# Seven products instead of eight in six of sixteen blocks of an MLP's second product

## The chip, the cores and the metric

The kernel runs on one NeuronCore of a Trainium2 chip. The metric is device time in microseconds for one execution. The core has a matrix engine (PE, TensorE), which reads its stationary and moving operands from on-chip SBUF and writes sums to one of eight PSUM banks of 128 x 512 float32 values; a vector engine (DVE, VectorE), a scalar engine (ACT, ScalarE) and a general one (POOL, GpSimd); and queues that move data from the chip's main memory (issued by SP here). Every engine takes its own instructions in order, and they wait for each other by semaphores.

## The reference

The program is a decoder of two layers on 256 tokens of width 1024. Each layer has attention (of two different kinds, which the change doesn't touch) and an MLP with a squared ReLU:

```
def rms_norm(x, g):
    y = x * rsqrt(mean(x * x, axis=-1) + 1e-5)
    return y * g

def sqrelu_mlp(x, w1, w2):
    h = relu(x @ w1)
    return (h * h) @ w2

h = h + attention(rms_norm(h, g0))
h = h + sqrelu_mlp(rms_norm(h, g1), w1, w2)
```

Here `w1` is 1024 x 4096 and `w2` 4096 x 1024, both float32, and the result is float32.

## The kernel before

**Products in three parts.** To keep float32 precision, every operand is split into a high part that PE takes at its fast rate (`float32r`) and a low part, the rest. A product is then three matmuls: high by high, high by low, low by high. `mm3` (L188 to L191) issues the three with the tokens stationary and 512 columns of weights moving. `wide` (L199) does the same with the weights stationary: one matmul of the high weights with 512 moving columns (256 tokens high, 256 tokens low) and one of the low weights with the 256 high tokens; the two halves of the PSUM bank are added afterwards.

**The stream of weights.** All weights of the program are entries of one list, `stream`, in the order of their use; an entry is 128 x 2048 values (1 MB). `fetch` (L101) loads an entry into one of three raw buffers, from SP's queue. `split` (L118) makes the high part (ScalarE, L135) and the low part (VectorE, L138) of half an entry, into one of three pairs of buffers `wh`, `wl`; so an entry takes the buffers of the entry three before it, when PE has read those for the last time. `W(i)` makes sure that entry i is split; `step()` splits one more half if it is at most two entries ahead of the current one. The MLP's entries alternate: first weights of block c, then second weights of block c - 1 (`feed_mlp`, L159).

**The MLP** (`mlp`, L302) goes over the 4096 hidden columns in 16 blocks of 256. For block c:
- the first product makes 256 hidden columns by 256 tokens: two halves f of 128 hidden columns, each summed over eight parts k of the width in a PSUM bank of its own, with 16 matmuls (`products`, L340).
- ScalarE copies one half of the bank to SBUF (L359) and VectorE adds the other (L360); VectorE squares with the ReLU (L363); ScalarE and VectorE make the high and low part `hh`, `hl` (L367, L368).
- the second product (`second`, L309) adds to four accumulators, token half t by output half n, each a PSUM bank of 512 columns: for each of them two products of blocks (f = 0, 1), so eight products or 24 matmuls.

The second product of block c - 1 follows the first of block c. The factor of the norm (one per token) is not applied in front: since relu(r x)^2 = r^2 relu(x)^2, the sums are multiplied by r^2 at the end, when they are added to the residual (`res`, L274, with `r2`). The last second products, those of blocks 14 and 15, run together, one accumulator after the other; `hook` adds each to the residual and starts what comes next.

**PSUM.** Four banks (`bank`) hold the accumulators, four (`bank2`) the first product of two blocks in turn.

**Order.** The program's text gives each instruction a priority; a planner orders each engine's instructions by priority and by its own estimate of when their inputs are ready. `tc.keep_in_program_order` holds an instruction to the text's order among those so held (PE's, where `strict[0]` is set), and `tc.high_priority` moves instructions forward.

The start of `mlp` is interleaved: half of the width is ready earlier, so blocks 0 and 1 begin with it (`begin`), then the other half of the tokens is transposed (`xt_tr`, L246), scaled and split (`xt_evac`, L256).

Of the kernel before, what the change touches and what calls it, by code (L numbers as in the profile page):

```python
# [62 lines left out]
def hybrid_kernel(ctx, tc, x, xca, xcb, eye, gcols, gfin, wqk, wva, wvb, wo0, wkv, wq, wg, rot, wo1, w1, w2, cw1, cw2, cpos, gate_b, cmask, consts, out):  # L63
# [9 lines left out]
    def f32(a):  # L73
        return a.bitcast(F32)
# [22 lines left out]
    ahead = [0]  # L97

    cur, at = [-1], [0, 0]

    def fetch():  # L101
# [16 lines left out]
    def split(pin=False):  # L118

        j, c = at  # L120
        src, n, plain = stream[j]
        if plain:

            made.append([wp.tile([P, n], F32, tag=f"w{a}", name="wc", bufs=3) for a in "hl"])
            for a in range(2):
                nc.sync.dma_start(made[j][a], src[a])
            at[:] = (j + 1, 0)
            return
        if c == 0:
            made.append((wp.tile([P, n], F32R, tag="wh", name="wh", bufs=3),  # L130
                         wp.tile([P, n], F32R, tag="wl", name="wl", bufs=3)))
        m = n // 4 if j < 2 else n // 2
        r = slice(c, c + m)
        h, lo = made[j]
        ins = nc.scalar.copy(h[:, r], raws[j][:, r])  # L135
        if pin:
            tc.keep_in_program_order(ins)
        nc.vector.tensor_sub(lo[:, r], raws[j][:, r], f32(h[:, r]))  # L138
# [49 lines left out]
    def mm3(o, a, b, first, last):  # L188
        pe(nc.tensor.matmul(o, a[0], b[0], start=first, stop=False, skip_group_check=True))  # L189
        pe(nc.tensor.matmul(o, a[0], b[1], start=False, stop=False, skip_group_check=True))  # L190
        pe(nc.tensor.matmul(o, a[1], b[0], start=False, stop=last, skip_group_check=True))  # L191
# [15 lines left out]
    def tok(xt, k, t):  # L207
        return xt[0][:, k, t * P:(t + 1) * P], xt[1][:, k, t * P:(t + 1) * P]
# [4 lines left out]
    def cut(hl, a, b):  # L213
        return hl[0][:, a:b], hl[1][:, a:b]
# [13 lines left out]
    def var_of(parts_):  # L228

        ss = sp.tile([P, 2], F32, name="ss")  # L230
        for i, src in enumerate(parts_):
            sq = sp.tile([P, D], F32, name="sq", tag="y")
            tc.keep_in_program_order(
                nc.scalar.activation(sq[:, 0:src.shape[1]], src, AF.Square, accum_out=ss[:, i:i + 1]))
# [3 lines left out]
        nc.vector.tensor_scalar(v, ss[:, 0:1], 1.0 / D, EPS, op0=OP.mult, op1=OP.add)  # L238
        return v

    def rstd_of(*parts_):
        r = sp.tile([P, 1], F32, name="r", bufs=4)
        nc.gpsimd.tensor_tensor(r, var_of(parts_), npow, op=OP.pow)
        return r
# [29 lines left out]
    def res(n, t, a, r=None, c=slice(0, 512)):  # L274
        hv = hres[t][:, n * 512 + c.start:n * 512 + c.stop]
        a = a[:, c]
        if r is None:
            nc.vector.tensor_add(hv, a, hv)
        else:
            nc.vector.scalar_tensor_tensor(hv, a, r, hv, op0=OP.mult, op1=OP.add)  # L280
# [21 lines left out]
    def mlp(layer, gi, xt, mid, ap):  # L302

        wa, wb = i_m[layer]
        acc = [[None, None], [None, None]]
        held = []
        r2 = []

        def second(items, order, hook=None):  # L309
            for i, (t, n, q) in enumerate(order):  # L310
                if hook is None and i % 2 == 0:
                    step()
                for c, hT, w in items:
                    for f in range(2):
                        if c == 0 and f == 0:
                            acc[n][t] = bank(f"acc{t}{n}")
                        if q.start and c == items[0][0] and f == 0:

                            acc[n][t] = bank2("accq")
                        o = f * D + n * 512  # L320
                        mm3(acc[n][t][:, q], tok(hT, f, t), cut(w, o + q.start, o + q.stop),
                            f == 0 and c == (items[0][0] if q.start else 0), c == NFC - 1 and f == 1)
                if hook is not None:
                    hook(i, t, n, q)

        whole = slice(0, 512)
        by_n = [(t, n, whole) for n in range(2) for t in range(T)]

        by_t = [(t, n, whole) for t in range(T) for n in range(2)][:-1] + [(1, 1, slice(0, 256)), (1, 1, slice(256, 512))]

        begun = {}

        def begin(c):

            w = W(wa[c])
            begun[c] = w, [bank2(f"pu{f}") for f in range(2)]
# [3 lines left out]
        def products(c, ks, done=None):  # L340
            w, pu = begun[c]
            for j, (f, k, i) in enumerate(ks):
                if j % 16 == 0 and (c or j):
                    step()
                wide(pu[f], cut(w, k * 256 + f * P, k * 256 + (f + 1) * P), xt, k, i, k == 0, k == NK - 1)
                if k == NK - 1 and i:
                    done(f, pu[f])

        def first(c):
            if c not in begun:  # L350
                begin(c)
            r = ap.tile([P, 512], F32, name="mr")
            u = ap.tile([P, 512], F32, name="mu")
            s = ap.tile([P, 512], F32, name="ms")

            def done(f, pu):

                q = slice(f * 256, (f + 1) * 256)
                nc.scalar.copy(r[:, q], pu[:, 256:512])  # L359
                nc.vector.tensor_add(u[:, q], pu[:, 0:256], r[:, q])  # L360

            products(c, [(f, k, i) for f in range(2) for i in range(2) for k in range(NK // 2 if c < 2 else 0, NK)], done)
            nc.vector.scalar_tensor_tensor(s, u, 0.0, u, op0=OP.max, op1=OP.mult)  # L363
            hh = ap.tile([P, 2, T * P], F32R, name="hh", bufs=3)
            hl = ap.tile([P, 2, T * P], F32R, name="hl", bufs=3)
            sv = s.rearrange("p (f q) -> p f q", f=2)
            nc.scalar.copy(hh, sv)  # L367
            nc.vector.tensor_sub(hl, sv, f32(hh))  # L368
# [7 lines left out]
        for c in range(NFC):  # L376
            hT = first(c)
            if c == 0:
                for t in range(T):
                    r = sp.tile([P, 1], F32, name="r2", bufs=4)  # L380
                    nc.vector.reciprocal(r, var_of([hres[t]]))
                    r2.append(r)
            if 0 < c < NFC - 1:
                second([held.pop(0) + (W(wb[c - 1]),)], by_n)
            held.append((c, hT))

        def hook(i, t, n, q):
            res(n, t, acc[n][t], r2[t], q if q.start else whole)
            mid(i, t, n, q)

        second([it + (W(wb[it[0]]),) for it in held], by_t if layer else by_n, hook)

    def layer0(ap):

# [714 lines left out]
```

## Time and profile before

| | us |
|---|---|
| three runs | 615.25, 616.37, 616.36 (median 616.36) |
| the profiled execution | 616.78 |
| its span, first to last instruction | 615.1 |
| MLP of layer 0, block 3 to the second product of block 13 | 144.33 to 276.64 |
| MLP of layer 1, the same | 459.50 to 591.84 |

The profile gives busy time by engine, and for each instruction its start, its length and what ended the idle time before it. A matmul's listed length (about 0.39 us for 512 columns) overlaps that of its neighbours; the distance of starts is what one costs. "L138" is a line of the kernel. In the groups by line the columns are busy time and mean length in ns, and behind the bar the engine's idle time ahead of these instructions with what ended it.

### The profile page before, as it was taken

What the parts mean: (1) busy time and instruction counts of PE and PEld (TensorE: products, weight loads), DVE (VectorE), ACT (ScalarE), POOL (GpSimd) and SP (SyncE); (2) the same over time, 40 slices, a digit from 0 to 9 for tenths busy, and PEclk for the clock granted to TensorE, in tenths of its full rate; (3) what the DMA queues carried; (4) which work ended last, traced back from release to release, by engine and by line L of the source; (5) the groups of instructions that cost most, each with busy time, mean ns of one, the idle gap of its engine ahead of it and who ended that gap; (6) DMA issues with size and microseconds to landing.
All of it is one profiled execution on the core that took longest, in us unless ns stands there. A gap on an engine that the chain in (4) does not pass through costs nothing.

```text
span 615.1 us, 8955 instructions
## 1 busy us (share of the span) xinstructions
PE 604.7 (98%) x3477; PEld 506.2 (82%) x3477; DVE 423.4 (69%) x692; ACT 342.4 (56%) x598; POOL 58.9 (10%) x81
## 2 busy tenths in 40 slices
PE   8999999999999999999999989999999999999995
PEld 5888887888888888888998778677888888888884
DVE  5588996876556665565797799755765665566655
ACT  6667765674553445443851698854654444444431
POOL 0201110000000000000330255440000000000000
PEclk9999999999999999999999999999999999999999
DMA  9963331655555455554486731211475555545501
GB/s 317 364 251 137 137 137 69 225 186 211 200 188 197 167 201 205 179 199 170 126 288 264 263 128 69 105 68 64 148 268 160 200 188 206 205 150 205 194 1 68
DMA packets 18810, 109.33 MB, mean 178 GB/s; under 512 B 2512, under 2 KB 3792, under 8 KB 6736
## 3 DMA queue, kind: packets, MB, share of 16 engines
q1 hardware_dynamic: 17472, 107.06, 48.2%
q10 hardware_dynamic: 1296, 1.70, 0.8%
q8 instruction: 27, 0.44, 0.3%
q14 instruction: 15, 0.12, 0.1%
HBM read 106.66 MB, written 1.05 MB: 175 GB/s over the span
## 4 chain that ended last, share of the span: by engine, by line
PE 90%; DVE 3%; DMA 2%; issue 2%; ACT 1%; SPq 0%; POOLq 0%; POOL 0%; DVEq 0%; ACTq 0%
PE pu L194 29%; PE acc L189 12%; PE acc L190 11%; PE acc L191 11%; PE qk L194 7%; PE po L194 3%; PE z L194 2%; PE pk L191 2%; PE pk L189 2%; PE pk L190 2%; DMA wc<-in_cw 2%; PE ptp L197 2%; PE pv L190 1%; PE pv L191 1%; DVE wl L138 1%
## 5 line engine op out<-in xcount | busy, mean ns | idle before, releaser
L138 DVE TENSOR_TENSOR wl<-raw,wh 128x1024 fp32r<-128x1024 f32 (+1 forms) x192 | 226.1, 1209 | 119.9 <-ACT wh L135 116.4
L135 ACT CAST wh<-raw 128x1024 fp32r<-128x1024 f32 (+1 forms) x192 | 190.9, 1033 | 107.3 <-PE acc L191 40.9
L194 PE MATMUL pu<-xn,wh 128*128 128x512 f32 x512 | 132.2, 392 | 0.0
L194 PEld LDWEIGHTS pu<-xn,wh 128*128 128x128 f32 x512 | 93.7, 188 | 18.0
L189 PE MATMUL acc<-wh,hh 128*128 128x512 f32 (+1 forms) x256 | 99.9, 390 | 0.0
L190 PE MATMUL acc<-wl,hh 128*128 128x512 f32 (+1 forms) x256 | 99.7, 389 | 0.0
L191 PE MATMUL acc<-wh,hl 128*128 128x512 f32 (+1 forms) x256 | 98.8, 388 | 0.0
L194 PE MATMUL pu<-xn,wl 128*128 128x256 f32 x512 | 76.5, 282 | 0.0
L194 PEld LDWEIGHTS pu<-xn,wl 128*128 128x128 f32 x512 | 72.1, 190 | 5.1
L191 PEld LDWEIGHTS acc<-wh,hl 128*128 128x128 f32 x256 | 48.1, 188 | 10.7 <-DVE hl L368 0.8
L189 PEld LDWEIGHTS acc<-wh,hh 128*128 128x128 f32 x256 | 48.2, 188 | 10.1 <-ACT hh L367 1.2
L190 PEld LDWEIGHTS acc<-wl,hh 128*128 128x128 f32 x256 | 48.2, 188 | 8.7
L367 ACT CAST hh<-ms 128x512 fp32r<-128x512 f32 x32 | 19.9, 621 | 63.0 <-DVE ms L363 63.0
L359 ACT COPY mr<-pu 128x256 f32<-128x256 f32 x64 | 23.6, 369 | 27.1 <-PE pu L194 27.1
L368 DVE TENSOR_TENSOR hl<-ms,hh 128x512 fp32r<-128x512 f32 x32 | 22.1, 691 | 19.2 <-ACT hh L367 19.2
L194 PE MATMUL qk<-xa,wh 128*128 128x512 f32 x128 | 32.5, 394 | 0.0
L360 DVE TENSOR_TENSOR mu<-pu,mr 128x256 f32<-128x256 f32 x64 | 26.6, 418 | 7.0 <-ACT mr L359 7.0
L887 POOL TENSOR_TENSOR pe<-pe,rs 128x512 f32<-128x512 f32 (+1 forms) x32 | 28.3, 917 | 25.5 <-DVE rs L882 13.6
L873 ACT ACTIVATE pe<-pe,nm 128x256 f32<-128x256 f32 (+1 forms) x64 | 28.3, 443 | 4.3 <-DVE nm L871 3.0
L194 PEld LDWEIGHTS qk<-xa,wh 128*128 128x128 f32 x128 | 22.9, 188 | 4.3 <-issue 0.2
L189 PE MATMUL acc<-wh,oT 128*128 128x512 f32 x64 | 26.3, 411 | 0.0
L190 PE MATMUL acc<-wl,oT 128*128 128x512 f32 x64 | 25.1, 392 | 0.0
(195 smaller groups left out, 827.2 us busy)
## 6 DMA issues: line engine op xcount, KB each, us to landing
raw<-in_w SPq DMA_DIRECT2D x64, 1024.0 KB, 4.8
raw<-in_wqk SPq DMA_DIRECT2D x8, 1024.0 KB, 5.1
raw<-in_wo SPq DMA_DIRECT2D x8, 1024.0 KB, 4.8
raw<-in_wkv SPq DMA_DIRECT2D x6, 1024.0 KB, 4.8
raw<-in_wq SPq DMA_DIRECT2D x4, 1024.0 KB, 5.0
wc<-in_cw SPq DMA_DIRECT2D x4, 1024.0 KB, 9.5
raw<-in_wvb SPq DMA_DIRECT2D x5, 512.0 KB, 7.1
raw<-in_wva SPq DMA_DIRECT2D x6, 256.0 KB, 5.2
```

What stands on the lines that cost most here:

```text
L135: ins = nc.scalar.copy(h[:, r], raws[j][:, r])
L138: nc.vector.tensor_sub(lo[:, r], raws[j][:, r], f32(h[:, r]))
L189: pe(nc.tensor.matmul(o, a[0], b[0], start=first, stop=False, skip_group_check=True))
L190: pe(nc.tensor.matmul(o, a[0], b[1], start=False, stop=False, skip_group_check=True))
L191: pe(nc.tensor.matmul(o, a[1], b[0], start=False, stop=last, skip_group_check=True))
L194: pe(nc.tensor.matmul(o, a, b, start=first, stop=last, skip_group_check=True))
L359: nc.scalar.copy(r[:, q], pu[:, 256:512])
L360: nc.vector.tensor_add(u[:, q], pu[:, 0:256], r[:, q])
L367: nc.scalar.copy(hh, sv)
L368: nc.vector.tensor_sub(hl, sv, f32(hh))
L873: nc.scalar.activation(e, e, AF.Exp, scale=-1.0, bias=nm[:, hd, t, b:b + 1], accum_out=rs[:, hd, t, b:b + 1])
L887: nc.gpsimd.tensor_tensor(sv, sv, rs[:, hd, t, :][:, :, None].to_broadcast([P, 2, n]), op=OP.mult)
```

## The change

Take the hidden values of a block as a 2 x 2 arrangement H (token half t, hidden half f) of 128 x 128 blocks and its second weights as W (hidden half f, output half n) of 128 x 512 blocks. In blocks 2, 4, 6, 8, 10 and 12 (`FEWER`) the product is formed with seven products of blocks (`fewer`) by Strassen's scheme in Winograd's form: four sums of hidden blocks (`hidden`) and four of weight blocks (`split` for entries in `mixed`, into `tx`, with high and low parts in `tp`) are made first. The seven products go to seven PSUM banks, `m` = 1 to 7. The other ten blocks still take eight products (`plain`), arranged so that they use four of these banks (2 to 5); for that they need two differences of hidden blocks.

What else changes with it:
- three of the seven accumulators take banks of the first product. From block 4 to block 14 its two halves share one bank, so the second product is cut into two parts and laid between the halves; `evac` copies the whole bank with ScalarE, in front by priority, and adds the halves from SBUF.
- the second product of a block runs later: its first part behind the next block's first product, its second part in the middle of the one after that. PE is held to the text's order from block 0's second half on.
- the factor of the norm is applied to the hidden values, since accumulators of several blocks are added into one another: `rstd_of` at the start of the MLP, broadcast by two matmuls (`pr`), and multiplied in `hidden` together with the ReLU; ScalarE squares. `res` adds without a factor.
- the first products of blocks 0, 1 and 2 run before any second product.
- `fold` adds banks 1, 6 and 7 to the residual after the last block with seven products.
- at the end, three accumulators take block 14's products before any takes block 15's.

The diff, cut to its core:

```
+FEWER = (2, 4, 6, 8, 10, 12)
...
@@ split
+        if j in mixed:
+            h, lo = made[j]
+            four = raws[j].rearrange("p (a q) -> p a q", q=512)
+            tx, th, tl = mixed[j]()
+            t4 = tx.rearrange("p (a q) -> p a q", q=512)
+            if c == 0:
+                nc.vector.tensor_sub(t4[:, 0:2, :], four[:, 1::2, :], four[:, 0:2, :])
+            else:
+                nc.vector.tensor_sub(t4[:, 2, :], four[:, 3, :], t4[:, 0, :])
+                nc.vector.tensor_sub(t4[:, 3, :], four[:, 2, :], t4[:, 2, :])
+            for dh, dl, src, r in ((h, lo, raws[j], slice(c, c + (1024 if c else 512))), (th, tl, tx, slice(c, c + 1024))):
+                nc.scalar.copy(dh[:, r], src[:, r])
+                nc.vector.tensor_sub(dl[:, r], src[:, r], f32(dh[:, r]))
...
@@ mlp
+        tp = pair([2048], "tp")
...
+        plain = ((2, 1, 0, 0), (2, 3, 0, 1024), (4, 0, 0, 0), (4, 2, 0, 1024),
+                 (5, 0, 0, 512), (5, 2, 0, 1536), (3, 4, 0, 512), (3, 5, 0, 1536))
+        fewer = ((1, 1, 0, 0), (2, 3, 0, 1024), (3, 7, 0, 1536), (4, 2, 1, 1536),
+                 (5, 4, 1, 0), (6, 5, 1, 1024), (7, 6, 1, 512))
...
+        def second(c, hT, part):
+            ps_ = fewer if c in FEWER else plain
+            for i, e in enumerate(ps_[:4] if part == 0 else ps_[4:]):
+                if i == 0:
                     step()
+                product(*e, hT, c)
...
+        def evac(c, f, pu):
+            if c not in parts:
+                parts[c] = ap.tile([P, 2, 512], F32, name="mr", bufs=1), ap.tile([P, 512], F32, name="mu")
+            r, u = parts[c]
+            with tc.high_priority(offset=300):
+                nc.scalar.copy(r[:, f, :], pu)
+            nc.vector.tensor_add(u[:, f * 256:(f + 1) * 256], r[:, f, 0:256], r[:, f, 256:512])
+
+        def hidden(c):
+            r, u = parts.pop(c)
+            few = c in FEWER
+            uv = u.rearrange("p (f q) -> p f q", f=2)
+            nc.vector.scalar_tensor_tensor(uv, uv, 0.0, rb[:, None, :].to_broadcast([P, 2, T * P]), op0=OP.max, op1=OP.mult)
+            hx = ap.tile([P, 8, P], F32, name="hx")
+            nc.scalar.activation(hx[:, 0:4, :].rearrange("p a q -> p (a q)"), u, AF.Square)
...
+            if few:
+                nc.vector.tensor_add(hx[:, 4], hx[:, 0], hx[:, 2])
+                nc.vector.tensor_sub(hx[:, 6], hx[:, 1], hx[:, 0])
+                nc.vector.tensor_sub(hx[:, 5], hx[:, 4], hx[:, 1])
+                nc.vector.tensor_sub(hx[:, 7], hx[:, 3], hx[:, 5])
+                r = slice(1, 8)
+            else:
+                nc.vector.tensor_sub(hx[:, 4:6], hx[:, 1:4:2], hx[:, 0:4:2])
+                r = slice(0, 6)
+            nc.scalar.copy(hh[:, r], hx[:, r])
+            nc.vector.tensor_sub(hl[:, r], hx[:, r], f32(hh[:, r]))
             return hh, hl
...
+        rs_ = [rstd_of(hres[t]) for t in range(T)]
+        products(0, rest)
+        products(1, rest[:8])
+        pr = bank("pr")
+        for t in range(T):
+            mm(pr[:, t * P:(t + 1) * P], rs_[t].to_broadcast([P, P]), ident, t == 0, True)
...
+        for c in range(3, NFC):
+            if c == 3:
+                pu = [zs[0], zs[2]]
+            elif c <= last_few + 2:
+                pu = [zs[0], zs[0]]
+            elif c % 2:
+                pu = [zs[0], zs[1]]
...
+            begun[c] = W(wa[c], keep=wb[done[0]] if done else None), pu
+            products(c, [(0, k, i) for i in range(2) for k in range(NK)])
+            if done and c < NFC - 1:
+                second(*done, 1)
+                if done[0] == last_few:
+                    fold()
+                W(wa[c])
+            products(c, [(1, k, i) for i in range(2) for k in range(NK)])
+            if c < NFC - 1:
+                second(*prev, 0)
+                done = prev
+            else:
+                second(*done, 1)
+                held.append(prev)
+            h = hidden(c)
+            prev = c, h
```

More of the change, by code (lines that the diff above doesn't have):

```diff
@@ L99, in hybrid_kernel @@
     cur, at = [-1], [0, 0]
+    mixed = {}
     def fetch():
@@ L304, in mlp @@
         wa, wb = i_m[layer]
[L305 to L311, printed above, removed]
-                    step()
[L313 to L336, printed above, removed]
+        tp = pair([2048], "tp")
+        tx = []
+        def sums():
+            if not tx:
+                tx.append(ap.tile([P, 2048], F32, name="tx", bufs=1))
+            return tx[0], tp[:, 0], tp[:, 1]
@@ new lines, in mlp, with product @@
+        for c in FEWER:
+            mixed[wb[c]] = sums
+        bank_of = {}
+        last_few = FEWER[-1]
+        plain = ((2, 1, 0, 0), (2, 3, 0, 1024), (4, 0, 0, 0), (4, 2, 0, 1024),
+                 (5, 0, 0, 512), (5, 2, 0, 1536), (3, 4, 0, 512), (3, 5, 0, 1536))
+        fewer = ((1, 1, 0, 0), (2, 3, 0, 1024), (3, 7, 0, 1536), (4, 2, 1, 1536),
+                 (5, 4, 1, 0), (6, 5, 1, 1024), (7, 6, 1, 512))
+        def product(m, a, kind, o, hT, c, q=slice(0, 512), o_bank=None, first=False):
+            w = W(wb[c])
+            if kind:
+                w = sums()[1:]
+            if o_bank is None:
+                first = m not in bank_of
+                if first:
+                    bank_of[m] = bank(f"acc{m}") if 2 <= m <= 5 else zs[{1: 1, 6: 3, 7: 2}[m]]
+                o_bank = bank_of[m]
+            mm3(o_bank[:, q], (hT[0][:, a, :], hT[1][:, a, :]), cut(w, o + q.start, o + q.stop), first,
+                c == NFC - 1 or c == last_few and m in (1, 6, 7))
@@ L341, in products @@
+        parts = {}
+        def products(c, ks):
             w, pu = begun[c]
@@ L346, in products @@
                 if k == NK - 1 and i:
[L347 to L368, printed above, removed]
-            return hh, hl
+                    evac(c, f, pu[f])
@@ L375, in mlp @@
         xt_evac(pt, 1, gi, xt)
[L376 to L388, printed above, removed]
-            mid(i, t, n, q)
@@ L391, in mlp @@
-        second([it + (W(wb[it[0]]),) for it in held], by_t if layer else by_n, hook)
+        strict[0] = True
+        rest = [(f, k, i) for f in range(2) for i in range(2) for k in range(NK // 2, NK)]
+        held = []
+        rb = ap.tile([P, T * P], F32, name="rb", bufs=1)
+        rs_ = [rstd_of(hres[t]) for t in range(T)]
[4 more added lines that the diff above has]
+            mm(pr[:, t * P:(t + 1) * P], rs_[t].to_broadcast([P, P]), ident, t == 0, True)
@@ new lines, in mlp @@
+        with tc.high_priority(offset=300):
+            nc.scalar.copy(rb, pr[:, 0:T * P])
+            first_two = [(0, hidden(0))]
+        products(1, rest[8:])
+        z1 = begun[1][1]
+        with tc.high_priority(offset=300):
+            first_two.append((1, hidden(1)))
+        begin(2, wb[0])
+        z0 = begun[2][1]
+        zs += [z0[0], z0[1], z1[0], z1[1]]
+        products(2, [(f, k, i) for f in range(2) for i in range(2) for k in range(NK)])
+        prev = 2, hidden(2)
+        for it in first_two:
+            second(*it, 0)
+            second(*it, 1)
@@ new lines, in mlp, with hook @@
+        held.append(prev)
+        strict[0] = False
+        def hook(i, t, n, q, a):
+            res(n, t, a, None, q if q.start else slice(0, 512))
+            if t == 0 and n == 1:
+                res(1, 1, a)
+            mid(i, t, n, q)
+        whole = slice(0, 512)
+        by_n = [(t, n, whole) for n in range(2) for t in range(T)]
+        by_t = [(t, n, whole) for t in range(T) for n in range(2)][:-1] + [(1, 1, slice(0, 256)), (1, 1, slice(256, 512))]
+        which = {(0, 0): plain[2:4], (0, 1): plain[4:6], (1, 0): plain[0:2], (1, 1): plain[6:8]}
@@ new lines, in mlp @@
+        order = by_t if layer else by_n
+        for t, n, q in order[:3]:
+            step()
+            for e in which[t, n]:
+                product(*e, held[0][1], held[0][0], q)
+        for i, (t, n, q) in enumerate(order):
+            es = which[t, n]
+            own = bank2("accq") if q.start else None
+            for c, hT in held[i < 3:]:
+                for e in es:
+                    product(*e, hT, c, q, own if own is not None else bank_of[e[0]], own is not None and c == held[0][0] and e is es[0])
+            hook(i, t, n, q, own if own is not None else bank_of[es[0][0]])
```

27 lines of the change are left out of this document (26 added, 1 removed).

## The prediction

> **What bounds the kernel now.** First the page: which engine is full, and the chain that ended last.
>
> ```profile
> PE 604.7 (98%) x3477; PEld 506.2 (82%) x3477; DVE 423.4 (69%) x692; ACT 342.4 (56%) x598; POOL 58.9 (10%) x81
> ...
> PE 90%; DVE 3%; DMA 2%; issue 2%; ACT 1%; SPq 0%; POOLq 0%; POOL 0%; DVEq 0%; ACTq 0%
> PE pu L194 29%; PE acc L189 12%; PE acc L190 11%; PE acc L191 11%; PE qk L194 7%; PE po L194 3%; PE z L194 2%; PE pk L191 2%; PE pk L189 2%; PE pk L190 2%; DMA wc<-in_cw 2%; PE ptp L197 2%; PE pv L190 1%; PE pv L191 1%; DVE wl L138 1%
> ```
>
> The chain is PE for 90%, and the MLP's two products are 63% of it (29 + 12 + 11 + 11). Busy shares alone could mislead, so the next view is the busy time by stretch: one block of layer 0's MLP, then eleven together.
>
> ```profile
> 177.41:188.44 11.03, 11.03 (x57) 9.42 (x56) 6.78 (x8) 5.27 (x7) 0.00 (x0) 1.00 0.56 191
> 155.36:276.64 121.28, 121.28 (x617) 103.63 (x616) 74.55 (x88) 57.97 (x77) 0.00 (x0) 1.00 0.54 191
> ```
>
> After length come PE, weight loads, VectorE, ScalarE, POOL, the clock and DMA. A block takes 11.03 us; PE has no idle time at full clock, VectorE works 6.78, ScalarE 5.27. A matmul taken away here is time taken away, until VectorE fills the 4.25 us that it has free. The timeline of that block gives the prices:
>
> ```profile
> 177.41 1.98 PE L194 MATMUL pu<-xn,wh 128*128 128x512 f32 x8
> 177.66 2.00 ACT L135 CAST wh<-raw 128x1024 fp32r<-128x1024 f32 x2 [1.26 <-PE acc L191]
> 178.74 2.36 DVE L138 TENSOR_TENSOR wl<-raw,wh 128x1024 fp32r<-128x1024 f32 x2 [1.62 <-ACT wh L135]
> 180.18 2.00 PE L194 MATMUL pu<-xn,wh 128*128 128x512 f32 x8
> 180.44 0.37 ACT L359 COPY mr<-pu 128x256 f32<-128x256 f32 x1 [0.77 <-PE pu L194]
> 182.97 0.40 PE L189 MATMUL acc<-wh,hh 128*128 128x512 f32 x1
> ...
> 187.46 0.69 DVE L368 TENSOR_TENSOR hl<-ms,hh 128x512 fp32r<-128x512 f32 x1 [0.69 <-ACT hh L367]
> 188.21 0.39 PE L191 MATMUL acc<-wh,hl 128*128 128x512 f32 x1
> 188.44 1.98 PE L194 MATMUL pu<-xn,wh 128*128 128x512 f32 x8
> ```
>
> Matmuls overlap, so their cost is the distance of starts. The 24 of the second product take 188.44 - 182.97 = 5.47 us, 0.228 each; one half of the first product (180.18 - 177.41) takes 2.77.
>
> **Removed.** One scalar product of blocks is three matmuls (L189 to L191). Seven instead of eight, in six blocks of two layers: 6 x 2 x 3 = 36 matmuls, 36 x 0.228 = **8.2 us**, all on PE's path. By the Trainium skill, "TensorE: Matmul & The Clock Gate", section "Wait — 56ns, not 53.3ns?", a warm 512-column matmul follows the last after 215.7 ns, which would make it 7.8 us; the rows above are 6% slower than that, and they decide.
>
> **Added on VectorE and ScalarE.** Prices by shape:
>
> ```profile
> L138 DVE TENSOR_TENSOR wl<-raw,wh 128x1024 fp32r<-128x1024 f32 x184 | 220.7, 1231 | 116.7 <-ACT wh L135 113.2 <-issue 3.4
> L135 ACT CAST wh<-raw 128x1024 fp32r<-128x1024 f32 x184 | 186.0, 1050 | 102.5 <-PE acc L191 40.9 <-PE pu L194 37.8 <-PE qk L194 6.1
> L360 DVE TENSOR_TENSOR mu<-pu,mr 128x256 f32<-128x256 f32 x64 | 26.6, 418 | 7.0 <-ACT mr L359 7.0
> L363 DVE SCALAR_TENSOR_TENSOR ms<-mu 128x512 f32<-128x512 f32 x32 | 22.1, 692 | 1.0
> L367 ACT CAST hh<-ms 128x512 fp32r<-128x512 f32 x32 | 19.9, 621 | 63.0 <-DVE ms L363 63.0
> L532 DVE TENSOR_TENSOR sbe<-sbe,sbs 128x774 f32<-128x774 f32 x8 | 7.7, 958 | 0.1
> L278 DVE TENSOR_TENSOR hres<-acc,hres 128x512 f32<-128x512 f32 x8 | 5.4, 683 | 2.8 <-PE acc L191 2.8
> L641 DVE TENSOR_TENSOR kv<-pk,rb 128x512 f32<-128x512 f32 x2 | 1.3, 682 | 0.0
> L761 ACT COPY hs<-ph 128x512 f32<-128x512 f32 x1 | 0.6, 587 | 0.0
> ...
> 332.82 0.26 DVE L716 TENSOR_TENSOR gates<-g 128x96 f32<-128x96 f32 x1
> 424.32 4.63 DVE L138 TENSOR_TENSOR wl<-raw,wh 128x1024 fp32r<-128x1024 f32 x4 [0.40 <-ACT wh L135]
> ```
>
> On VectorE 96, 256, 512, 774 and 1024 columns lie on one line of 0.15 us plus 1.04 ns a column; so 128 columns cost 0.29, 768 cost 0.95 and 896 cost 1.08 (estimates from these rows). A broadcast operand (L641) costs nothing extra. Blocks with seven products (even) and with eight (odd) alternate, so I count a pair:
> - weights of the even block: three differences of weight blocks (1.23 + 0.69 + 0.69), the low part of 1536 columns (0.69 + 1.23), the low part of the sums (2 x 1.23): 6.99 us, seven instructions
> - its hidden values: scale 0.69, four sums of 128 columns 1.16, low part of 896 columns 1.08: 2.93, six instructions
> - the odd block: weights 2.46, hidden values 0.69 + 0.42 + 0.95 = 2.06, five instructions
> - first weights and halves added, both blocks: 4 x 1.23 + 4 x 0.42 = 6.60, eight instructions
>
> Sum **21.0 us** in 26 instructions. PE needs 2 x 11.03 - 3 x 0.228 = **21.4** for the pair. But queued neighbours overlap: four of 1.231 take 4.63 (L138, at 424.32), 0.10 less at each junction, so VectorE may need as little as 21.0 - 2.6 = 18.4. Its load is therefore between 86% and 98% of PE's, against 61% now. I take 91%, since most of its queue is full then, though what waits for its own neighbour doesn't overlap. ScalarE: nine casts of 1024 columns 9.45, one of 512 0.62, four copies of a bank at 0.59, two squares 1.24, casts of 896 and 768 columns about 1.8 (between 0.62 and 1.05 each): 15.5, or 72%; it has room.
>
> **Where it is tightest.** Each weight entry takes the buffer of the entry three before it. In the new order (half a first product, 2.77; the older block's second half; the other half; the newer block's first half, 2.73) VectorE has from the end of the older block's second half to the seven-product block's first use: 2.77 + 2.73 + 2.77 + 2.73 + 2.77 = 13.8 us. In it fall one first weight (2.46), two additions (0.84), the hidden values (2.93) and the even weights (6.99): 13.2 in durations, some 11.8 with overlap, and one cast (1.05) before the first can start, which the weight differences can fill as they need raw weights alone. Late by 13.2 + 1.05 - 13.8 = 0.45 us per pair at worst, early at best: 0 to 5.4 us over 12 pairs. I take 1.0.
>
> **The single bank.** Seven accumulators leave one bank for the first product from block 4 to 14. Its copy now stands between PE's blocks: 44 handovers (per layer six behind nine matmuls, 2.05 us; sixteen behind twelve, 2.73). The copy starts 0.26 after PE goes on (180.44 against 180.18) and takes 0.59: done at 0.85, so one cast of 1.05 may stand in front even in the short ones. Cost nothing, hidden behind the second product; if it slips, see the rivals.
>
> **Start of a layer.** The scale is needed early now:
>
> ```profile
> 300.85 1.06 ACT L234 ACTIVATE sq<-hres 128x1024 f32<-128x1024 f32 x1
> 302.04 0.15 DVE L238 TENSOR_SCALAR v<-ss 128x1 f32<-128x1 f32 x1 [0.43 <-ACT sq L234]
> 302.27 0.55 POOL L243 TENSOR_TENSOR r<-v,cst 128x1 f32<-128x1 f32 x1 [1.24 <-DVE v L238]
> ...
> 121.47 0.48 DVE L263 SCALAR_TENSOR_TENSOR xn<-pt,gc,xn 128x256 fp32r<-128x256 f32 x1 [0.15 <-ACT xn L262]
> 127.67 1.55 PE L194 MATMUL pu<-xn,wh 128*128 128x512 f32 x6
> ...
> L194 PE MATMUL pr<-ident,r 128*128 128x128 f32 x8 | 1.2, 274 | 0.0
> ```
>
> Square to power is 302.27 + 0.55 - 300.85 = 2.0 us, 3.2 with the first token half's square. Counted from 121.5 it ends at 124.7; PE reaches the broadcast after the rest of block 0 and half of block 1's, 2.8 + 1.4 us behind 122, at 126.3: no wait. The matmuls themselves: 1.2 / 8 x 4 = 0.6 us. Three first products run before any second, so block 2's weights are due at 128, in the buffer that block 0 frees at 124.9. Now PE also starts six of them at 127.67, but turns to a second product after that; then it must go on, while ScalarE also has the hidden values to cast. 0 to 1.5 us a layer, I take 0.4: 0.8.
>
> **End of a layer.**
>
> ```profile
> 286.71 0.19 PEld L189 LDWEIGHTS acc<-wh,hh 128*128 128x128 f32 x1 [0.43 <-ACT hh L367]
> 287.44 0.19 PEld L191 LDWEIGHTS acc<-wh,hl 128*128 128x128 f32 x1 [0.20 <-DVE hl L368]
> ```
>
> PE waits 0.63 us for the last hidden values. Eighteen matmuls of block 14 (4.1 us) go ahead of them now, so that wait goes; but the last second weights wait for a buffer that block 13 now frees only after the last first product, and come due 4.1 us later: cast and low part of both halves, 2.00 + 1.2 plus queueing. Between -0.6 and +1.0 a layer, I take 0. The fold (six additions of 0.683 and a copy of 0.587) lies in block 14 beside 10.3 us of PE, with block 15's lighter work to catch up in. The new addition at the end (0.68) is ahead of the last matmuls.
>
> **Sum.** -8.2 + 1.0 + 0.6 + 0.8 = -5.8 us. The profiled run took 616.8 us (span 615.1); the median of the three shown is 616.4, 0.4 under it. So 616.4 - 5.8 = **610.6 us**. Nothing lost and the end's wait gained, -8.2 + 0.6 - 0.9 = -8.5: 607.9.
>
> **Rivals.**
> 1. The handover. ScalarE runs in order; two casts in front of the bank's copy make 0.26 + 2.1 + 0.59 = 2.95 us, late by 0.9 in the short handovers and 0.22 in the long. At all 44 that is 12 x 0.9 + 32 x 0.22 = 17.8 us; at one in three 5.9, and the gain is gone: 616.5. At one in eight, 612.8. For it: ScalarE's queue waits for buffers that PE frees (1.26 at 177.66), and what stands behind waits too. Against it: 72% load, and the copy is given priority in the order.
> 2. VectorE becomes the bound: **slower**. If neighbours don't overlap, it has 21.0 us of work a pair; with two waits of 0.69 as at 187.46 left bare (one per block, hl behind hh) it takes 22.4, against 22.06 of PE now: 0.36 x 12 = 4.3 slower, with the starts 1.4 more: 622.1. It decides from 0.9 us of bare waits a pair on. For it: VectorE idles 4.25 of 11.03 us now, waiting for ScalarE. Against it: it waits with nothing else to do, and the sums need only raw weights, so they can fill it; and the 4.63 us above. The Trainium skill, "VectorE: DVE Perf Modes", section "The DRAIN you can't avoid", says that the next instruction doesn't start until the pipe is empty. By that rule the 21.0 stands and this rival would be the likely one; the 4.63 for four of 1.231 speaks against it here.
>
> **Chances.** Forecast (607.9 to 612.8) 0.65; handovers slip in few places (to 615.2) 0.12; in about a third, no change, 0.08; VectorE bound 0.15. A measurement of this kernel tells about 0.2% (1.2 us) from no change. Faster 0.77, same 0.08, slower 0.15. The range takes the first two cases: 607.9 to 615.2.
>
> **What would show it.** Right: 36 fewer 128x512 matmuls; pairs of blocks near 21.4 us; PE without waits for wh, hh or mr; VectorE near 19.5 us a pair. Rival 1 shows as PE waits for ACT mr of 0.2 to 0.9 us behind each half, rival 2 as VectorE without idle time and PE waiting for DVE wl or hl. A late scale shows as PE waiting before pr. I am wrong if pairs take over 21.8 us, or a layer's start costs more than 1.5.

## The result, and the profile after

The changed kernel takes **611.39 us** (median of 4 runs, 610.89 to 611.75); the kernel before took 616.22 beside it (4 runs, 615.25 to 616.37). The ratio is 0.9925, with a 95% interval of 0.9913 to 0.9937: 0.75% faster. The forecast was 610.6 in a range of 607.9 to 615.2.

The page of the changed kernel first: busy time by engine, then the chain that ended last, and two groups of section 5.

```profile
PE 598.4 (98%) x3449; PEld 501.0 (82%) x3449; DVE 503.4 (83%) x830; ACT 397.8 (65%) x658; POOL 61.2 (10%) x85
...
PE 91%; DVE 3%; DMA 2%; issue 2%; ACT 1%; POOLq 0%; POOL 0%; DVEq 0%; ACTq 0%
...
L158 DVE TENSOR_TENSOR wl<-raw,wh 128x1024 fp32r<-128x1024 f32 (+1 forms) x168 | 199.7, 1210 | 43.2 <-ACT wh L155 39.6
...
L389 ACT COPY mr<-pu 128x512 f32<-128x512 f32 x64 | 37.2, 581 | 15.7 <-PE pu L214 15.7
```

PE still bounds the kernel (91% of the chain). It lists 28 matmuls fewer: 36 gone from the second product, 8 new ones (L214, `pr`). VectorE has taken on 80 us of work and ScalarE 55.

The busy time by stretch comes next: two pairs of blocks (one with seven products, one with eight), then blocks 4 to 14. The columns are length, PE, weight loads, VectorE, ScalarE, POOL, clock, DMA share and GB/s.

```profile
183.99:205.47 21.48, 21.48 (x111) 18.27 (x110) 19.28 (x27) 14.25 (x18) 0.00 (x0) 1.00 0.51 196
205.47:226.95 21.48, 21.48 (x111) 18.28 (x110) 19.29 (x27) 14.25 (x18) 0.00 (x0) 1.00 0.54 196
...
151.95:269.75 117.80, 117.80 (x599) 100.26 (x598) 106.22 (x146) 77.82 (x99) 0.00 (x0) 1.00 0.54 199
```

A pair takes 21.48 us instead of 2 x 11.03 = 22.06, PE has no idle time in it, VectorE works 19.28 us (90%) and ScalarE 14.25 (66%). The list of PE's waits over the whole kernel has nothing from the MLP:

```profile
PE warm L214 <- DVE zero L237: 1.2, 1, 1.2
PE pss L214 <- DVE kcb L905: 1.0, 1, 1.0
PE ph L214 <- DMA wc<-in_cw: 0.6, 1, 0.6
PE ptp L217 <- POOL pe L1002: 0.6, 1, 0.6
PE z L214 <- DVE qkT L621: 0.2, 1, 0.2
```

Where the 5.79 us between the two profiled spans lie (starts of matmuls read from the two traces; the end is that of the last instruction):

| stretch | before | after | difference |
|---|---|---|---|
| start to the MLP of layer 0 | 115.57 | 114.33 | -1.24 |
| MLP 0, first matmul to the next stage's first | 178.79 | 175.92 | -2.87 |
| attention of layer 1 | 136.38 | 136.75 | +0.37 |
| MLP 1, first matmul to the last start | 177.72 | 174.84 | -2.88 |
| last start of a matmul to the end | 6.60 | 7.43 | +0.83 |

The first row is code that the change doesn't touch; its first matmul of `qk` began at 28.46 us in the one profile and 27.27 in the other, and at 27.2 to 28.2 in the other kernels below. It belongs to the executions. Without it the rows give -4.55, near the difference of the medians (-4.83).

### The profile page after: what moved, and what is told of

It is laid out like the page before. It is cut to its first block, busy times and chain, and to the rows that moved or that the text cites. A ratio compares the mean times of both kernels' runs of the same rounds, so it can differ in the third digit from the quotient of the medians.

```text
span 609.3 us, 9115 instructions
## 1 busy us (share of the span) xinstructions
PE 598.4 (98%) x3449; PEld 501.0 (82%) x3449; DVE 503.4 (83%) x830; ACT 397.8 (65%) x658; POOL 61.2 (10%) x85
## 4 chain that ended last, share of the span: by engine, by line
PE 91%; DVE 3%; DMA 2%; issue 2%; ACT 1%; POOLq 0%; POOL 0%; DVEq 0%; ACTq 0%
PE pu L214 29%; PE acc L209 10%; PE acc L211 10%; PE acc L210 10%; PE qk L214 7%; PE po L214 3%; PE z L214 2%; PE pk L209 2%; PE pk L211 2%; PE pk L210 2%; DMA wc<-in_cw 2%; PE ptp L217 2%; PE pu L211 1%; PE pu L210 1%; PE pu L209 1%
## 5 line engine op out<-in xcount | busy, mean ns | idle before, releaser
L158 DVE TENSOR_TENSOR wl<-raw,wh 128x1024 fp32r<-128x1024 f32 (+1 forms) x168 | 199.7, 1210 | 43.2 <-ACT wh L155 39.6
L214 PE MATMUL pu<-xn,wh 128*128 128x512 f32 x512 | 131.5, 391 | 0.0
L214 PEld LDWEIGHTS pu<-xn,wh 128*128 128x128 f32 x512 | 95.1, 188 | 19.5 <-DVE xn L283 0.2
L214 PE MATMUL pu<-xn,wl 128*128 128x256 f32 x512 | 76.5, 282 | 0.0
L214 PEld LDWEIGHTS pu<-xn,wl 128*128 128x128 f32 x512 | 72.0, 190 | 5.1
L211 PE MATMUL acc<-wh,hl 128*128 128x512 f32 (+1 forms) x184 | 72.3, 393 | 0.0
L210 PE MATMUL acc<-wl,hh 128*128 128x512 f32 (+1 forms) x184 | 72.0, 391 | 0.0
L209 PE MATMUL acc<-wh,hh 128*128 128x512 f32 (+1 forms) x184 | 72.0, 391 | 0.0
L389 ACT COPY mr<-pu 128x512 f32<-128x512 f32 x64 | 37.2, 581 | 15.7 <-PE pu L214 15.7
L411 DVE TENSOR_TENSOR hl<-hx,hh 128x768 fp32r<-128x768 f32 (+1 forms) x32 | 32.1, 1004 | 6.9 <-ACT hh L410 6.9
L146 ACT CAST tp<-tx 128x1024 fp32r<-128x1024 f32 x24 | 25.2, 1049 | 18.9 <-DVE tx L141 17.7
L398 ACT ACTIVATE hx<-mu 128x512 f32<-128x512 f32 x32 | 20.2, 630 | 24.3 <-DVE mu L396 24.3
L410 ACT CAST hh<-hx 128x768 fp32r<-128x768 f32 (+1 forms) x32 | 28.1, 877 | 8.1 <-DVE hx L408 7.8
L214 PE MATMUL qk<-xa,wh 128*128 128x512 f32 x128 | 32.5, 394 | 0.0
L390 DVE TENSOR_TENSOR mu<-mr 128x256 f32<-128x256 f32 x64 | 26.8, 420 | 5.7 <-ACT mr L389 5.7
L988 ACT ACTIVATE pe<-pe,nm 128x256 f32<-128x256 f32 (+1 forms) x64 | 28.2, 442 | 4.4 <-DVE nm L986 3.3
L147 DVE TENSOR_TENSOR tp<-tx,tp 128x1024 fp32r<-128x1024 f32 x24 | 29.2, 1218 | 0.0
```

The lines of the kernel that those rows point to most:

```text
L147: nc.vector.tensor_sub(dl[:, r], src[:, r], f32(dh[:, r]))
L214: pe(nc.tensor.matmul(o, a, b, start=first, stop=last, skip_group_check=True))
L389: nc.scalar.copy(r[:, f, :], pu)
L410: nc.scalar.copy(hh[:, r], hx[:, r])
L411: nc.vector.tensor_sub(hl[:, r], hx[:, r], f32(hh[:, r]))
L988: nc.scalar.activation(e, e, AF.Exp, scale=-1.0, bias=nm[:, hd, t, b:b + 1], accum_out=rs[:, hd, t, b:b + 1])
```

## The experiments

"After" is the changed kernel; each edit is made to it.

**Where the gain is: eight products everywhere, and three blocks of six.**

```
-FEWER = (2, 4, 6, 8, 10, 12)
+FEWER = ()
...
-                if done[0] == last_few:
-                    fold()
```

> The changed kernel with no block at seven products: all sixteen take eight, everything else of the change stays (norm in front, shared bank, second product later and in two parts); no sums of weights, no fold. If the gain is the 36 matmuls that go: 36 x 0.228 = 8.2 us slower than the changed kernel, 619.6, and so 3.4 slower than the kernel before, which is then the price of the rest of the change. Rival, the gain comes from the new order or the norm in front and the matmuls were hidden: 611 to 613.

Measured 619.52 us (619.32 to 619.94) against 616.10: ratio 1.0059, interval 1.0044 to 1.0074. With `FEWER = (4, 8, 12)` alone:

> The changed kernel with seven products in three blocks of each layer (4, 8, 12) instead of six. If PE is the bound throughout, half of the matmuls come back: 18 x 0.228 = 4.1 us, 615.5. If VectorE or the shared bank already limits the six, taking three away costs less than that: 612 to 614.

Measured 615.55 us (615.13 to 615.88), ratio 0.9992 (0.9983 to 1.0001). From none to 18 to 36 matmuls gone the time falls by 3.97 and 4.16, against 18 x 0.228 = 4.1. The two MLPs alone, read from the traces, say it more sharply: that of layer 0 (first matmul to the next stage's first) takes 180.00, 177.96 and 175.92 us with none, three and six such blocks, that of layer 1 178.92, 176.88 and 174.84, so 2.04 for every nine matmuls, 0.227 each. The matmuls are worth what their spacing says, and the sums that replace them cost nothing: the kernel with no sums at all loses 3.4 us to the kernel before, and that loss is all that the one with six blocks of sums has given away too (8.2 - 4.8 = 3.4). The cost lies in what stands around the scheme (order, norm in front, end): without sums the two MLPs are 1.21 and 1.20 longer than before, and the end 0.84.

**The handover of the shared bank.**

```
-            with tc.high_priority(offset=300):
-                nc.scalar.copy(r[:, f, :], pu)
+            nc.scalar.copy(r[:, f, :], pu)
```

> The changed kernel without the priority of ScalarE's copy of the first product's bank. If ScalarE's load (66%) leaves the copy in time anyway: no change, 611.4. Rival, the handover hangs on the priority: two casts in front of the copy make PE late by 0.9 us in the 12 short handovers and 0.2 in the 32 long ones, up to 17.8 us slower; a third of them 5.9, 617.

Measured 610.66 us (610.56 to 611.10), ratio 0.9917 (0.9903 to 0.9930). The two traces list the same instructions in the same order on every engine: the planner puts the copies there without the priority too. So this run measures after a second time and doesn't show what a late copy costs. Both MLPs last as long as after's (175.90 and 174.84 in its trace); the 0.7 us less lie in the attention of layer 1 (136.03 instead of 136.75), where after's wait of PE `ph` for the DMA of `wc` (0.6) is missing. What speaks against rival 1 is after's own trace: PE waits nowhere for the copy, and in blocks 4 to 14 of layer 0 each copy ends 0.71 us or more before PE starts the next half in that bank.

**How much room VectorE has.** The first attempt put needless 128x1024 subtractions of a constant into each block with seven products, one and three:

```
+                spare = ap.tile([P, 1024], F32, name="spare", bufs=1)
+                for _ in range(3):
+                    nc.vector.tensor_sub(spare, ballast, ballast)
```

> The changed kernel with one needless subtraction of 128x1024 on VectorE in each block of seven products. Next to neighbours it is 1.14 us (1.22 less the overlap), so VectorE goes from 19.3 to 20.4 us of a pair's 21.5. If PE bounds with VectorE in its shadow: within 0.6 us of the changed kernel, 611.4 to 612. If VectorE is the bound already: 12 x 1.14 = 13.7 us slower, 625.

> The same with three needless subtractions: VectorE 19.3 + 3.4 = 22.7 us against 21.5 of PE. If neighbours overlap as the trace of the changed kernel shows, VectorE becomes the bound with 1.2 us a pair over, plus its 0.5 us or so of waits that can't be filled: 12 x 1.2 to 1.7, 14 to 20 us slower, 626 to 632. If something else holds the pair at 21.5, no change.

Measured 612.66 (611.02 to 612.80) and 612.65 us (611.82 to 613.55), ratio 0.9947 for both (0.9931 to 0.9964, 0.9932 to 0.9961). The run with one came out 0.7 us over its forecast, the run with three 13 under. The view of the tile in the latter (count, length, first and last start):

```profile
L410 DVE TENSOR_TENSOR spare<-ballast x36: 1209/1219/1226, 108.5 to 546.1; 128x1024 f32<-128x1024 f32 x36
```

The first starts at 108.5, ahead of the MLP (115.1): their input is ready from the beginning, so the planner is free to move them. In the run with one, a single subtraction of layer 0 (at 158.4) lies in blocks 4 to 14, so it tells nothing of the bound. In the run with three the moving explains little of the miss: 13 of layer 0's 18 start in these blocks, and VectorE has hardly a gap left:

```profile
152.00:270.00 118.00, 117.72 (x598) 99.91 (x597) 117.67 (x157) 78.10 (x99) 0.00 (x0) 1.00 0.53 195
```

Yet blocks 4 to 14 take only 118.36 us (from 152.84 to 271.20) instead of 117.80. The second attempt reads hidden values of the block itself, which holds each subtraction to its place:

```
+            if few:
+                spare = ap.tile([P, 8, P], F32, name="spare", bufs=1)
+                for _ in range(1):
+                    nc.vector.tensor_sub(spare, hx, hx)
```

> As e3, but the needless subtraction of 128x1024 reads the block's hidden values, so it can't be moved out of the MLP: one in each block of seven products. VectorE 19.3 + 1.14 = 20.4 of 21.5 us a pair. If PE bounds and VectorE is in its shadow up to the full pair: within 0.6 us of the changed kernel, 611.4 to 612. If VectorE's order and waits leave no room in practice: up to 13.7 us slower, 625.

> The same with three: VectorE 19.3 + 3.4 = 22.7 of 21.5 us. VectorE is then the bound with 1.2 us a pair over (eleven blocks in a row ran it at 99%, so with hardly any waits): 11 to 12 pairs, 13 to 15 us slower than the changed kernel, 624 to 627. If VectorE doesn't bound there: 611 to 613.

One subtraction: 611.02 us (610.52 to 611.58), ratio 0.9923 (0.9909 to 0.9938). Three: 615.41 (615.01 to 617.00), ratio 0.9995 (0.9985 to 1.0004). A pair of blocks, then blocks 4 to 14, of the run with one:

```profile
184.70:206.18 21.48, 21.48 (x111) 18.28 (x109) 20.33 (x28) 14.24 (x18) 0.00 (x0) 1.00 0.54 196
152.82:270.62 117.80, 117.80 (x600) 100.27 (x598) 111.45 (x151) 77.81 (x99) 0.00 (x0) 1.00 0.54 198
```

Blocks 4 to 14 of the run with three, and PE's largest wait in that kernel:

```profile
152.73:272.79 120.06, 118.74 (x599) 100.01 (x598) 119.48 (x158) 78.59 (x99) 0.00 (x0) 1.00 0.54 193
...
PE acc L210 <- DVE wl L147: 2.6, 6, 0.5
```

With 20.33 us of VectorE's work in a pair of 21.48 nothing waits, and the stretch is as long as after's (117.80). With three, VectorE has no gap left (119.48 of 120.06), PE starts to wait for `wl`, and the stretch is 2.26 us longer. By pairs, the first and the fourth of that run:

```profile
152.73:174.21 21.48, 21.48 (x110) 18.28 (x109) 21.26 (x29) 14.62 (x19) 0.00 (x0) 1.00 0.54 196
217.76:240.08 22.32, 21.82 (x110) 18.20 (x109) 22.21 (x30) 14.36 (x18) 0.00 (x0) 1.00 0.53 187
```

The first two pairs take 21.48 us as in after, although VectorE is full in them; the next three take 22.07, 22.32 and 22.31, about as long as VectorE works. So the bound of rival 2 is there, at VectorE's full load, but it comes late. These rows fit a lead that the first pairs use up (halves of weights are split up to two entries ahead of the current one); the lead itself was not measured. The size was missed (624 to 627 expected) because that reckoning charged 1.2 us to every pair, and three pairs of layer 0 paid 0.6 to 0.8.

**Every block from 2 to 12 with seven products.** Two consecutive blocks then need sums, so the second gets buffers of its own:

```
-FEWER = (2, 4, 6, 8, 10, 12)
+FEWER = tuple(range(2, 13))
...
+            if c % 2 == 0:
+                return tx[0], tp[:, 0], tp[:, 1]
+            if not other:
+                other.extend(big([P, 2048], F32R, f"tp{a}") for a in "hl")
+            return tx[0], other[0], other[1]
```

> Seven products in all eleven blocks from 2 to 12, with a second buffer for the sums of weights; sums still on VectorE. PE would save 30 more matmuls, 6.8 us: 604.6. But VectorE has per block 2.46 + 0.84 + 2.93 + 6.99 = 13.2 us in durations, about 12 with overlap, against 10.4 of PE: if VectorE then bounds, a block takes about 12.1 instead of 10.74, 22 x 1.36 = 30 us slower, 641 (range 625 to 650). If it comes out faster, VectorE is not what limits the number of blocks.

The same, with the sums of weight blocks on GpSimd (`nc.gpsimd.tensor_sub(t4...)`):

> The same eleven blocks with the three differences of weight blocks on POOL, which is idle in the MLP. 2048 columns at 2.3 ns each (512 in 1.16 us in the attention of layer 1) are 4.7 us of 10.4 a block. VectorE keeps 13.2 - 2.6 = 10.6 in durations, 9.3 with overlap, 89% of PE, as now. If the same arithmetic holds: PE bounds again, 604.6 to 606. If POOL's work slows VectorE's or comes too late for the casts: 611 or more.

The first took 625.95 us (624.76 to 627.19), ratio 1.0164 (1.0149 to 1.0179), inside its range and 15 below its middle. Blocks 4 to 14 by windows, PE's largest waits over the kernel, and the group that the next paragraph needs:

```profile
152.86:277.63 124.77, 118.34 (x585) 96.36 (x583) 124.05 (x181) 84.52 (x108) 0.00 (x0) 1.00 0.50 182
...
PE acc L210 <- DVE tp L147: 4.3, 6, 0.8
PE acc L210 <- DVE tpl L147: 3.9, 6, 0.7
PE acc L210 <- DVE wl L147: 3.1, 5, 1.0
...
L147 DVE TENSOR_TENSOR wl<-raw,wh 128x1024 fp32r<-128x1024 f32 x10 | 12.2, 1218 | 0.0
```

VectorE is full (124.05 of 124.77), PE waits for it, and thirty matmuls fewer than after cost 15 us more. Here rival 2 is the result: slower than the kernel before. It comes late here too. From the start of block 4 and from that of block 10 to the next block's:

```profile
152.86:163.26 10.40, 10.40 (x54) 8.86 (x53) 10.40 (x16) 8.02 (x11) 0.00 (x0) 1.00 0.56 198
219.69:231.47 11.78, 10.98 (x54) 8.70 (x53) 11.78 (x18) 7.89 (x10) 0.00 (x0) 1.00 0.47 180
```

Blocks 4 to 6 take PE's 10.40 each, block 7 10.62, blocks 8 to 13 from 11.76 to 12.57, around the 12.1 of the forecast. So its price of a block was right, and its 22 blocks that pay it were too many.

The second took 693.30 us (693.18 to 694.49), ratio 1.1264 (1.1246 to 1.1281). The forecast's second case (611 or more) holds, with 82 us above its figure. Its windows, groups by shape over blocks 4 to 14, and rows from the timelines of GpSimd and of VectorE:

```profile
155.80:311.64 155.84, 129.85 (x585) 103.01 (x583) 146.92 (x159) 85.21 (x110) 56.42 (x27) 0.93 0.42 156
...
L147 DVE TENSOR_TENSOR wl<-raw,wh 128x1024 fp32r<-128x1024 f32 x10 | 29.9, 2988 | 0.0
L395 DVE TENSOR_TENSOR mu<-mr 128x256 f32<-128x256 f32 x24 | 18.8, 782 | 0.0
...
175.13 2.16 POOL L143 TENSOR_TENSOR tx<-raw,tx 128x512 f32<-128x512 f32 x1
177.37 1.35 POOL L144 TENSOR_TENSOR tx<-raw,tx 128x512 f32<-128x512 f32 x1
...
176.05 1.51 DVE L395 TENSOR_TENSOR mu<-mr 128x256 f32<-128x256 f32 x1
177.60 1.67 DVE L401 SCALAR_TENSOR_TENSOR mu<-mu,rb 128x512 f32<-128x512 f32 x1
...
182.39 0.42 DVE L395 TENSOR_TENSOR mu<-mr 128x256 f32<-128x256 f32 x1
```

VectorE lost 22 instructions in this stretch and got busier (146.92 us against 124.05), while GpSimd is at work for only 56 us. The means hide two cases. Of the 24 additions of halves 16 have no GpSimd instruction beside them and take 417 ns, as in the run before; the other 8 take 1513. Of the ten subtractions of L147 shown, eight run beside GpSimd and take about 3430 ns, the other two 1213. The rows of the timelines show what happens: the addition at 176.05 ends at 177.56, 0.27 us after GpSimd's instruction beside it (177.29), and the same addition alone takes 0.42 (182.39); the next one ends at 179.27, 0.55 after GpSimd's (178.72). The Trainium skill, "SBUF — State Buffer", section "Who interferes with whom", says that a VectorE instruction with two inputs in SBUF contends with a GpSimd instruction that reads SBUF, and that their shared ports are an exclusive lock; these rows agree, and it makes GpSimd no place for work that is to unload VectorE here. The handover of the bank slips as well in this run: over these blocks PE waits 20.2 us for the copy `mr`, the sign of rival 1.

**The end of the kernel.** The addition that the change put behind the second accumulator of the last block is moved into block 15, and the last two blocks are arranged so that its bank is finished by then:

```
...
-            if t == 0 and n == 1:
-                res(1, 1, a)
...
                 second(*done, 1)
+                res(1, 1, bank_of[5])
...
-(1, 1): plain[6:8]}
+(1, 1): ((3, 1, 0, 512), (3, 3, 0, 1536))}
```

> The changed kernel with the last two blocks' share of token half 1, output half 1 taken by two direct products into bank 3, and bank 5 as it stands after block 13 added to that residual before block 14 adds to it; so the extra addition of 128x512 leaves the end. The tail behind the last matmul has grown by 0.84 us (7.43 against 6.60). If that addition is why: 0.7 to 0.9 faster than the changed kernel, 610.6. If the tail's growth has another cause: no change.

Measured 612.12 us (611.59 to 612.57), ratio 0.9940 (0.9927 to 0.9952): no gain in total. In its trace the stretch from the last matmul's start to the end is 6.98 instead of 7.43, so the edit gives 0.45 back; this trace lost more in the attention of layer 1 (137.82 instead of 136.75), where PE waits 1.6 us for the DMA of `wc` instead of 0.6.

**The order inside the first product.** Its sixteen matmuls of a half (eight of 512 columns, then eight of 256) take turns, from block 3 on:

```
-            products(c, [(0, k, i) for i in range(2) for k in range(NK)])
+            products(c, [(0, k, i) for k in range(NK) for i in range(2)])
```

> From block 3 on, the eight 512-column matmuls of a half of the first product and its eight 256-column ones take turns instead of standing in two rows; nothing else differs. In the trace of the changed kernel the 256-column ones are 120 ns apart and the twelve 512-column ones behind such a row 228 to 241 ns instead of 226.7, so twelve take 2.77 us instead of 2.72 and nine 2.09 instead of 2.04, at four places a pair of blocks. Theory A, the row of short matmuls causes it (it uses up a lead that the weight loads had, 188 ns each against 120): without rows the twelve take 2.72 to 2.73, a half still 2.77 or less, about 0.10 us a pair less, 1.2 us over 12 pairs: 609.9 to 610.4. Theory B, it belongs to the second product and its operands whatever stands ahead: the spacing stays and the time is 611.4. Theory C, the low parts of the first weights are now due 1.7 us earlier and VectorE, at 90% already, brings them late: PE waits for DVE wl in front of 256-column matmuls, and the time is over 612.

Measured 613.58 us (612.66 to 614.36), ratio 0.9952 (0.9935 to 0.9969). PE's timeline in this run, at the start of a part of the second product and behind it:

```profile
187.79 0.39 PE L209 MATMUL acc<-wh,hh 128*128 128x512 f32 x1
...
190.57 0.39 PE L214 MATMUL pu<-xn,wh 128*128 128x512 f32 x1
190.80 0.28 PE L214 MATMUL pu<-xn,wl 128*128 128x256 f32 x1
...
191.26 0.40 PE L214 MATMUL pu<-xn,wh 128*128 128x512 f32 x1
191.50 0.28 PE L214 MATMUL pu<-xn,wl 128*128 128x256 f32 x1
...
193.38 0.39 PE L209 MATMUL pu<-wh,hh 128*128 128x512 f32 x1
```

Twelve matmuls of the second product still take 190.57 - 187.79 = 2.78 us, and the half of the first product now 193.38 - 190.57 = 2.81 instead of 2.77, since what follows a 512-column matmul now starts up to 240 ns behind it there as well (191.50 - 191.26). Theory A falls, and PE waits for nothing in the MLP, so theory C does too. B's spacing stayed, but its time (611.4) didn't: 52 halves (blocks 3 to 15, two layers) at 0.04 more are 2.1 of the 2.2 us.

**Two blocks of three with seven products.** Six blocks leave VectorE at 90%, eleven overfill it, so eight, with the second set of buffers:

```
-FEWER = (2, 4, 6, 8, 10, 12)
+FEWER = (2, 3, 5, 6, 8, 9, 11, 12)
```

> Seven products in eight blocks (2, 3, 5, 6, 8, 9, 11, 12), with a second buffer for the sums of weights. VectorE: a block of seven products takes 11.3 us of it (eleven blocks in a row: 124.1 / 11), one of eight 19.3 - 11.3 = 8.0; three blocks 30.6. PE: 21.48 / 2 + 0.34 = 11.08 for a block of eight, 10.40 for one of seven, three 31.9. VectorE at 96%, so PE should still bound: 4 blocks x 0.68 = 2.7 us faster than the changed kernel, 608.7. If two such blocks in a row are late because their sums crowd together: 611 to 614.

Measured **608.05 us** (607.81 to 608.40), ratio 0.9874 (0.9858 to 0.9891): faster than both kernels. Blocks 4 to 14:

```profile
152.70:269.14 116.44, 116.44 (x593) 99.12 (x592) 112.51 (x159) 81.32 (x102) 0.00 (x0) 1.00 0.56 204
```

VectorE is at 97% and PE still has no wait in the MLP. This doesn't live on a lead: the first nine of these blocks take 31.88 us in each group of three, and VectorE works 30.64 and 30.62 in the second and third. Twelve matmuls fewer than after gave 3.3 us: 12 x 0.228 = 2.7 in the two MLPs (1.36 a layer in this stretch), the rest in the attention of layer 1, which took 135.94 without a wait for `wc`.

## Why the prediction was right, and where its terms were off

- **Removed, 8.2 us: right.** 0.228 a matmul, shown by the kernels with none, three and six such blocks (4.0 and 4.2 for 18 each, 0.227 a matmul in the traces).
- **VectorE's load: right.** Forecast 91% and near 19.5 us a pair, measured 90% and 19.28. Neighbours overlap as the row of before said; the timeline of after has the same:

```profile
190.66 3.50 DVE L158 TENSOR_TENSOR wl<-raw,wh 128x1024 fp32r<-128x1024 f32 x3 [1.26 <-ACT wh L155]
```

  Three of 1.22 take 3.50. By the rule of the Trainium skill that was weighed there ("VectorE: DVE Perf Modes", section "The DRAIN you can't avoid") they would take 3.66 and a pair about 21.0; the measurements decide against that rule here. The same section of the Trainium skill adds an exception that the prediction left out, that a next operation which isn't held starts earlier; these rows agree with the exception. ScalarE came to 14.25 us a pair, under the 15.5 of the sum.
- **1.0 us for VectorE's lateness: wrong in its cause, near in size by luck.** PE never waits for it; 1.1 us more work a pair (the run with one subtraction tied to its place) is free as well. The pair is 21.48 instead of 21.38 for another reason: the second product's matmuls are further apart. Starts in PE's timeline of after at the end of layer 0, where over 30 follow one another:

```profile
275.31 0.39 PE L209 MATMUL acc<-wh,hh 128*128 128x512 f32 x1
...
276.23 0.40 PE L210 MATMUL acc<-wl,hh 128*128 128x512 f32 x1
276.46 0.40 PE L211 MATMUL acc<-wh,hl 128*128 128x512 f32 x1
276.70 0.40 PE L209 MATMUL acc<-wh,hh 128*128 128x512 f32 x1
```

  Six take 276.70 - 275.31 = 1.39 us, 232 ns each, and it goes on so; before, 24 took 5.47, 228 each, with 226 to 227 from the sixth on. At 0.10 us a pair and six pairs a layer it makes 1.2 us. The kernel with eight products everywhere has it too; in its timeline a part of twelve, between two halves of the first product, takes 196.45 - 193.68 = 2.77:

```profile
193.68 0.39 PE L209 MATMUL acc<-wh,hh 128*128 128x512 f32 x1
...
196.45 1.98 PE L214 MATMUL pu<-xn,wh 128*128 128x512 f32 x8
```

  So neither the sums nor the seven products cause it, and the run with turns shows that the row of short matmuls ahead doesn't either. What does stays open.
- **`pr` and the start, 1.4 together: 1.0.** From the MLP's first matmul to block 3 it is 28.76 -> 29.29 in layer 0 and 28.78 -> 29.23 in layer 1. PE didn't wait ahead of `pr`, as forecast.
- **The bank's handover at nothing: right** (no wait for `mr`, and 0.71 us or more to spare in blocks 4 to 14 of layer 0).
- **The end at nothing: the step that failed.** The end of a layer cost 0.1 to 0.2 each (what is left of the MLPs' difference), but from the last matmul to the end 0.83 us came on. The step read "the new addition at the end (0.68) is ahead of the last matmuls". It is, and that doesn't hide it. VectorE's timeline of after at the end; the last matmul starts at 601.84:

```profile
596.49 0.69 DVE L298 TENSOR_TENSOR hres<-acc,hres 128x512 f32<-128x512 f32 x1 [1.82 <-PE acc L211]
...
597.88 0.69 DVE L298 TENSOR_TENSOR hres<-acc,hres 128x512 f32<-128x512 f32 x1
598.49 0.14 DVE L1105 TENSOR_SCALAR ssq<-ssq 128x1 f32<-128x1 f32 x1
598.55 0.68 DVE L298 TENSOR_TENSOR hres<-acc,hres 128x512 f32<-128x512 f32 x1
599.15 0.74 DVE L1107 CUSTOM_DVE_ANT_0 ys<-hres,ssq 128x512 f32<-128x512 f32 x1
...
602.01 0.68 DVE L298 TENSOR_TENSOR hres<-acc,hres 128x512 f32<-128x512 f32 x1
...
603.13 0.42 DVE L298 TENSOR_TENSOR hres<-accq,hres 128x256 f32<-128x256 f32 x1
```

  The same place in the trace of before, where the last matmul starts at 608.46:

```profile
601.82 0.75 DVE L280 SCALAR_TENSOR_TENSOR hres<-acc,r,hres 128x512 f32<-128x512 f32 x1 [1.28 <-PE acc L191]
...
607.53 0.74 DVE L280 SCALAR_TENSOR_TENSOR hres<-acc,r,hres 128x512 f32<-128x512 f32 x1
...
608.78 0.48 DVE L280 SCALAR_TENSOR_TENSOR hres<-accq,r,hres 128x256 f32<-128x256 f32 x1
```

  After, VectorE works in a row from its first `hres` to 604.08; before, it has one gap, 0.66 us for GpSimd's `r` at 605.47. The first `hres` is 608.46 - 601.82 = 6.64 us ahead of the last matmul before, and 601.84 - 596.49 = 5.35 after, since three accumulators have block 14's products by then and little PE work is left behind the first. So the addition of the last bank starts 0.17 behind the last matmul instead of 0.93 ahead of it. From the first `hres` to it are 5.71 us before and 5.52 after, with the new addition (598.55) among them; without that one they are 5.05 (602.97 - 597.92 in the run above), which gave 0.45 of the 0.83 back. The rest is put down to the shorter cover by these rows, without a run for it.
- **Sum.** In the two MLPs -8.2 and 2.45 lost (1.0 start, 1.2 spacing, 0.25 ends), -5.75, against -5.8 forecast; the 0.8 us between forecast and median are of the size of the end. The attention's 0.37 lies inside what its wait for `wc` varies between kernels (135.9 to 137.8).
- **Rival 2** had the right mechanism and, with six blocks, too high a load (21.0 us a pair against 19.28 measured). It decides when VectorE has no gap left (99.5% of the stretch with three subtractions tied to their place, 99.4% with eleven blocks), and then not at once: the first two pairs or three blocks of layer 0 still go at PE's pace, and the later ones take about as long as VectorE works.

## What to carry to other kernels

Where one engine is full and another has room, price the trade in the first engine's spacing, and load the second up to shortly before its gaps are used up (the best point here, 608.05 us, has it at 97%). Beyond that, look at the iterations one by one and not at the stage's sum: the first ones can hide an overload by work done ahead, and only the later ones show what it costs, so a short stage looks better than a long one would. What stands "ahead of the last matmul" is hidden only if its engine has a gap between there and the end. To load an engine on purpose, make the added work depend on data of the place it is meant for, or some of it will be moved. And where a run with an edit comes out as before, look whether the order of instructions has changed at all.

## What the runs showed of the hardware that was not expected

- GpSimd beside VectorE: with both inputs in SBUF, a 128x256 addition of VectorE took 417 ns alone and 1513 beside a subtraction on GpSimd, a 128x1024 subtraction 1213 alone and about 3430 beside one. GpSimd's own 128x1024 subtractions took 2748 ns in the mean.
- Matmuls of the same listed shape keep two spacings, 226 to 227 ns in the first product's rows and about 231 (228 to 241) in the rewritten second product, at full granted clock and without a wait; behind 512-column ones that stand between 256-column ones the next start is up to 240 later. The cause is open.
